# Row kurtosis of a 1024 x 8192 matrix: unequal folded groups replaced by 32 equal groups in a hand-set order

## The chip, the cores and the metric

The kernel runs on one core of one Trainium2 chip. The time is device time in microseconds (us) of one execution; three executions of the kernel before were timed, and one more was profiled.

## The reference

For each of the 1024 rows of x (8192 numbers, float32) the kernel returns the excess kurtosis.

```python
mean = np.mean(x, axis=-1, keepdims=True)
std = np.std(x, axis=-1, keepdims=True)
z = (x - mean) / (std + 1e-8)
return (np.mean(z ** 4, axis=-1) - 3).astype(np.float32)
```

Both kernels compute, per row, the mean, then S2, the sum of (x - mean)^2, then S4, the sum of (x - mean)^4, and return n * S4 / S2^2 - 3. The addition of 1e-8 is left out in both.

## The kernel before, in words

A group is a set of rows that fills the 128 partitions. With a fold of k, each row is cut in k pieces that lie on k neighbouring partitions, so that a group has 128/k rows and its tile is 128 x (8192/k). PLAN (line 15) lists the 24 groups in order: folds 8, 8, 4, then thirteen groups of fold 2 (64 rows, tile 128 x 4096, 2 MB), then 4, 4, 8, 8, 16, 16, 16, 16. Each group passes through these steps:

- one load of the whole tile from SP's queue (line 188), into one of a few slots for its width (10 for fold 2);
- the mean. For folds 4 and more, VectorE adds up each partition (line 96) and TensorE adds the pieces of a row with a block matrix (line 103). For fold 2, TensorE transposes the tile in 128 x 128 pieces, all accumulated into one PSUM tile `tps` (line 123: 32 matmuls for a tile of 4096 columns), VectorE adds the k neighbours and spreads the sum over them in one reduction to `red` (line 129, which reads each value k times), and TensorE adds over the partitions with a column of -1/n (line 134);
- ScalarE copies the negative mean `nmu` from PSUM (lines 105, 137);
- ScalarE squares (x + nmu) in place and sums into a column of `sa` (line 192), followed by its own read of the accumulator. This is called the square below;
- the fourth power: a square of the square with a sum, on VectorE (line 175), or on ScalarE (line 171) for every fifth group (groups 2, 7, 12, 17, 22); half each for the last group.

Groups of one fold that stand next to each other form a batch (six of them). At the end of a batch two sums over the pieces go through TensorE (`p2`, `p4`, lines 151 to 153), four small VectorE instructions form the result (lines 155 to 160), and it is stored, from ScalarE's queue but for the last batch.

The order of the instructions on each engine is set by the framework's scheduler and not by the code: it places the next group's transposes, for instance, partly ahead of line 134 of the group before. `psum` has two buffers of `tps` and of `mps`, `psfin` one of `p2` and of `p4`.

Of the kernel before, what the change touches and what calls it, by code (L numbers as in the profile page):

```python
# [7 lines left out]
f32 = mybir.dt.float32  # L8
bf16 = mybir.dt.bfloat16
AO = mybir.AluOpType  # L10
AF = mybir.ActivationFunctionType
P = 128


PLAN = [8, 8, 4, 2, 2, 2, 2, 2, 2, 2, 2, 2, 2, 2, 2, 2, 4, 4, 8, 8, 16, 16, 16, 16]
SLOTS = {2: 10, 4: 2, 8: 2, 16: 4}


@with_exitstack
def kernel(  # L20
    ctx: ExitStack,
    tc: tile.TileContext,
    x: bass.AP,
    out: bass.AP,
):
    nc = tc.nc
    n_rows, n_cols = x.shape
    neg_inv_n = -1.0 / float(n_cols)
    assert sum(P // k for k in PLAN) == n_rows

    xpool = ctx.enter_context(tc.tile_pool(name="xpool", bufs=1))
    const = ctx.enter_context(tc.tile_pool(name="const", bufs=1))
    junkp = ctx.enter_context(tc.tile_pool(name="junkp", bufs=1))
    small = ctx.enter_context(tc.tile_pool(name="small", bufs=6))
    fin = ctx.enter_context(tc.tile_pool(name="fin", bufs=2))
    psum = ctx.enter_context(tc.tile_pool(name="psum", bufs=2, space=bass.MemoryType.PSUM))
    psfin = ctx.enter_context(tc.tile_pool(name="psfin", bufs=1, space=bass.MemoryType.PSUM))


    warm = const.tile([P, 1], f32, name="warm")  # L40
    nc.vector.memset(warm, 0.0)
    nc.scalar.activation(out=warm, in_=warm, func=AF.Square)


    blk = {}

    def block_matrix(k):
        if k not in blk:
            r = P // k
            b = const.tile([P, P], f32, name=f"blk{k}")  # L50
            v = b.rearrange("p (r k) -> p r k", k=k)
            nc.gpsimd.memset(b, neg_inv_n)
            nc.gpsimd.affine_select(  # L53
                out=v, in_=v, pattern=[[-k, r], [0, k]], base=0,
                channel_multiplier=1, compare_op=AO.is_ge, fill=0.0,
            )
            nc.gpsimd.affine_select(  # L57
                out=v, in_=v, pattern=[[k, r], [0, k]], base=k - 1,
                channel_multiplier=-1, compare_op=AO.is_ge, fill=0.0,
            )  # L60
            blk[k] = b
        return blk[k]

    for k in PLAN:
        block_matrix(k)

    groups = []
    row = 0
    for k in PLAN:
        groups.append((row, k, P // k, n_cols // k))  # L70
        row += P // k


    batches = []
    for i, g in enumerate(groups):
        if batches and groups[batches[-1][0]][1] == g[1] and len(batches[-1]) < 64:
            batches[-1].append(i)
        else:
            batches.append([i])
    where = {}  # L80
    for b in batches:
        n = len(b)
        sa = const.tile([P, 2 * n], f32, name=f"sa{b[0]}")
        sd = const.tile([P, n], f32, name=f"sd{b[0]}")
        nc.gpsimd.memset(sa, 0.0)
        nc.gpsimd.memset(sd, 0.0)
        for j, i in enumerate(b):
            where[i] = (b, j, n, sa, sd)

    junk = junkp.tile([P, 1024], bf16, name="junk")  # L90

    def mean_dve(i, xt):
        row, k, r, w = groups[i]
        h = w // 2
        part = small.tile([P, 1], f32, name="part")
        nc.vector.tensor_tensor_reduce(  # L96
            out=junk[:, :h], in0=xt[:, :h], in1=xt[:, h:],
            scale=neg_inv_n if k == 1 else 1.0, scalar=0.0,
            op0=AO.add, op1=AO.add, accum_out=part)
        if k == 1:  # L100
            return part
        mps = psum.tile([P, 1], f32, name="mps")
        nc.tensor.matmul(mps, lhsT=blk[k], rhs=part, start=True, stop=True)  # L103
        nmu = small.tile([P, 1], f32, name="nmu")
        nc.scalar.copy(nmu, mps)  # L105
        return nmu

    ident = const.tile([P, P], f32, name="ident")
    nc.gpsimd.memset(ident, 1.0)
    nc.gpsimd.affine_select(  # L110
        out=ident, in_=ident, pattern=[[-1, P]], base=0,
        channel_multiplier=1, compare_op=AO.is_equal, fill=0.0)
    negcol = const.tile([P, 1], f32, name="negcol")
    nc.gpsimd.memset(negcol, neg_inv_n)

    def mean(i, xt):
        row, k, r, w = groups[i]
        if k > 2:
            return mean_dve(i, xt)
        ch = w // P  # L120
        tps = psum.tile([P, P], f32, name="tps")
        for c in range(ch):
            nc.tensor.matmul(tps, lhsT=xt[:, c * P:(c + 1) * P], rhs=ident,  # L123
                             start=c == 0, stop=c == ch - 1, is_transpose=True)
        red = small.tile([P, P], f32, name="red")
        if k == 1:
            nc.vector.tensor_copy(red, tps)
        else:
            nc.vector.tensor_reduce(  # L129
                out=red.rearrange("p (r k) -> p r k", k=k),  # L130
                in_=tps.rearrange("p (r k) -> p r k", k=k).unsqueeze(2).to_broadcast([P, r, k, k]),
                op=AO.add, axis=mybir.AxisListType.X)
        mps = psum.tile([P, 1], f32, name="mps")
        nc.tensor.matmul(mps, lhsT=red, rhs=negcol,  # L134
                         start=True, stop=True)
        nmu = small.tile([P, 1], f32, name="nmu")
        nc.scalar.copy(nmu, mps)  # L137
        return nmu

    def split(i, w):  # L140
        if i == len(groups) - 1:
            return w // 2
        return w if i % 5 == 2 else 0

    def finish_batch(b):
        _, _, n, sa, sd = where[b[0]]
        row, k, r, w = groups[b[0]]
        sel = blk[k].rearrange("p (r k) -> p r k", k=k)[:, :, 0]
        p2 = psfin.tile([n, r], f32, name="p2")
        p4 = psfin.tile([n, r], f32, name="p4")  # L150
# [3 lines left out]
        rec = fin.tile([n, r], f32, name="rec")
        nc.vector.reciprocal(rec, p2)  # L155
        kr = fin.tile([n, r], f32, name="kr")
        nc.vector.scalar_tensor_tensor(  # L157
            out=kr, in0=p4, scalar=-1.0, in1=rec, op0=AO.mult, op1=AO.mult)
        nc.vector.tensor_mul(kr, kr, rec)  # L159
        nc.vector.tensor_scalar_add(kr, kr, -3.0)  # L160
        dst = out[row:row + n * r].rearrange("(g r) -> g r", r=r)
        eng = nc.sync if b is batches[-1] else nc.scalar
        eng.dma_start(out=dst, in_=kr)  # L163

    def fourth(i):
        row, k, r, w = groups[i]
        b, j, n, sa, sd = where[i]
        xt = tiles[i]
        cl = split(i, w)
        if cl > 0:  # L170
            nc.scalar.activation(  # L171
                out=xt[:, :cl], in_=xt[:, :cl], func=AF.Square,
                accum_out=sa[:, n + j:n + j + 1])
        if cl < w:
            nc.vector.tensor_tensor_reduce(  # L175
                out=xt[:, cl:], in0=xt[:, cl:], in1=xt[:, cl:], scale=1.0, scalar=0.0,
                op0=AO.mult, op1=AO.add, accum_out=sd[:, j:j + 1])
        if j == n - 1:
            finish_batch(b)

    tiles = {}
    used = {}
    for i, (row, k, r, w) in enumerate(groups):
        s = used.get(w, 0)
        used[w] = s + 1
        xt = xpool.tile([P, w], f32, name=f"x{k}", tag=f"x{k}_{s % SLOTS[k]}")
        tiles[i] = xt
        nc.sync.dma_start(
            out=xt, in_=x[row:row + r, :].rearrange("r (k w) -> (r k) w", k=k))
        nmu = mean(i, xt)  # L190
        b, j, n, sa, sd = where[i]
        nc.scalar.activation(  # L192
            out=xt, in_=xt, func=AF.Square, bias=nmu, accum_out=sa[:, j:j + 1])
        if i > 0:
            fourth(i - 1)
    fourth(len(groups) - 1)


# [28 lines left out]
```

## Time and profile before

| what | value |
|---|---|
| median of the three timed runs | 134.7 us (134.06 to 134.92) |
| the profiled execution: its own time | 134.22 us |
| span of that execution, first to last instruction | 132.5 us |
| busy: VectorE (DVE) | 73.6 us, 56% |
| busy: ScalarE (ACT) | 80.2 us, 61% |
| busy: TensorE (PE), matmuls | 74.8 us, 56% |
| loaded from HBM | 33.55 MB |

The span is part of the execution's own time; 1.72 us lie around it. Busy shares are means over stages that differ, so the rows below go by stages and by single steps. PEclk is the clock that TensorE was granted, 1.00 for 2.4 GHz and 0.50 for 1.2 GHz.

### The profile page before, as it was taken

The numbers are of one execution on the slowest core, as the hardware profiler recorded it, in microseconds if no ns is written. First come the engines' busy times: TensorE is split into PE (matmuls) and PEld (weight loads), VectorE is DVE, ScalarE is ACT, GpSimd is POOL, SyncE is SP. The second block draws the span as 40 slices with busy tenths as digits, with TensorE's granted clock in tenths as the row PEclk, the third lists the DMA queues.
The fourth block names the chain that finished last, engine by engine and source line by source line (L and its number), as shares of the span: only waits on it lengthen the run. The fifth ranks groups of instructions, "written<-read, shape, count | busy, mean of one in ns | idle before, by whom it ended". The sixth has DMA issues, their size and how long they took to land. (4 is left out here: it accounts for less than half of the span.)

```text
span 132.5 us, 1379 instructions
## 1 busy us (share of the span) xinstructions
PE 74.8 (56%) x500; PEld 69.0 (52%) x500; DVE 73.6 (56%) x98; ACT 80.2 (61%) x86; POOL 5.8 (4%) x31
## 2 busy tenths in 40 slices
PE   0223999419894298789403989168999202115430
PEld 0221989319794297779303979067989101014420
DVE  0458011580299709610996069931015999998881
ACT  4076608309292196999901948047899694449890
POOL 8900000000000000000000000000000000000000
PEclk9999999985699959999995599965589975555555
DMA  4999999999999999999999996000000000000000
GB/s 114 433 462 415 420 445 401 425 435 401 465 406 450 415 435 435 401 460 406 455 406 406 419 403 232 0 2 0 0 0 7 0 0 0 0 0 1 0 0 0
DMA packets 3511, 33.64 MB, mean 254 GB/s; under 512 B 433, under 2 KB 433, under 8 KB 1457
## 3 DMA queue, kind: packets, MB, share of 16 engines
q1 hardware_dynamic: 3464, 33.56, 60.5%
q8 instruction: 4, 0.07, 0.2%
q14 instruction: 3, 0.02, 0.0%
q10 hardware_dynamic: 40, 0.00, 0.0%
HBM read 33.55 MB, written 0.00 MB: 253 GB/s over the span
## 5 line engine op out<-in xcount | busy, mean ns | idle before, releaser
L175 DVE CUSTOM_DVE_ANT_0 x<-x 128x4096 f32<-128x4096 f32 (+4 forms) x19 | 57.4, 3027 | 10.1 <-ACT x L192 5.0
L192 ACT ACTIVATE x<-x,nmu 128x4096 f32<-128x4096 f32 (+3 forms) x24 | 61.7, 2573 | 1.3 <-DVE kr L160 0.6
L123 PE MATMUL tps<-ident,x 128*128 128x128 f32 x416 | 61.2, 318 | 0.3 <-DMA x<-in_x_dram 0.3
L123 PEld LDWEIGHTS tps<-ident,x 128*128 128x128 f32 x416 | 59.6, 172 | 0.4 <-issue 0.4
L129 DVE TENSOR_REDUCE red<-tps 128x128 f32<-128x256 f32 x13 | 5.5, 423 | 38.2 <-PE tps L123 38.2
L137 ACT COPY nmu<-mps 128x1 f32<-128x1 f32 x13 | 2.0, 155 | 36.0 <-PE mps L134 36.0
L134 PE MATMUL mps<-negcol,red 128*128 128x1 f32 x26 | 5.5, 282 | 27.4 <-DVE red L129 27.4
L134 PEld LDWEIGHTS mps<-negcol,red 128*128 128x128 f32 x26 | 4.7, 225 | 30.5 <-issue 19.1
L171 ACT ACTIVATE x<-x 128x2048 f32<-128x2048 f32 (+3 forms) x6 | 12.1, 2013 | 0.9 <-DVE rec L155 0.8
L103 PE MATMUL mps<-part,blk 128*128 128x1 f32 x22 | 6.1, 358 | 10.5 <-DVE part L96 10.5
L103 PEld LDWEIGHTS mps<-part,blk 128*128 128x128 f32 x22 | 5.4, 315 | 11.6 <-issue 7.7
L96 DVE CUSTOM_DVE_ANT_0 junk<-x 128x512 bf16<-128x512 f32 (+2 forms) x11 | 8.1, 737 | 5.7 <-DMA x<-in_x_dram 5.7
L105 ACT COPY nmu<-mps 128x1 f32<-128x1 f32 x11 | 1.4, 153 | 10.4 <-PE mps L103 10.4
L151 PE MATMUL p<-blk,sa 128*2 128x16 f32 (+4 forms) x12 | 1.6, 218 | 10.4 <-ACT x L192 8.7
L151 PEld LDWEIGHTS p<-blk,sa 128*2 128x2 f32 (+3 forms) x12 | 0.6, 85 | 11.0 <-ACT x L192 9.1
L153 PE MATMUL p<-blk,sd 128*2 128x16 f32 (+4 forms) x12 | 1.6, 222 | 5.4 <-DVE sd L175 5.3
L192 ACT ACTIVATION_READ_ACCUMULATOR x<-x,nmu 128x1 f32 x24 | 4.5, 187 | 0.0
L153 PEld LDWEIGHTS p<-blk,sd 128*2 128x2 f32 (+3 forms) x12 | 0.8, 92 | 5.7 <-DVE sd L175 4.0
L57 POOL TENSOR_SCALAR_AFFINE_SELECT blk<-blk 128x128 f32<-128x128 f32 x4 | 2.1, 545 | 0.0
L155 DVE RECIPROCAL rec<-p 2x16 f32<-2x16 f32 (+4 forms) x6 | 1.9, 317 | 0.3 <-PE p L151 0.2
L152 PE MATMUL p<-blk,sa 128*2 128x16 f32 (+4 forms) x12 | 1.5, 206 | 1.0 <-ACT x L171 0.8
L53 POOL TENSOR_SCALAR_AFFINE_SELECT blk<-blk 128x128 f32<-128x128 f32 x4 | 1.9, 501 | 0.0
(20 smaller groups left out, 11.5 us busy)
## 6 DMA issues: line engine op xcount, KB each, us to landing
x<-in_x_dram SPq DMA_DIRECT2D x13, 2048.0 KB, 27.9
x<-in_x_dram SPq DMA_DIRECT2D x3, 1024.0 KB
x<-in_x_dram SPq DMA_DIRECT2D x4, 512.0 KB, 3.9
x<-in_x_dram SPq DMA_DIRECT2D x4, 256.0 KB, 14.4
out_dram<-kr ACTq DMA_DIRECT2D x3, 0.1 KB
out_dram<-kr ACTq DMA_DIRECT2D x1, 3.2 KB
out_dram<-kr ACTq DMA_DIRECT2D x1, 0.2 KB
out_dram<-kr SPq DMA_DIRECT2D x1, 0.1 KB
```

The costliest lines, as they stand in the source:

```text
L57: nc.gpsimd.affine_select(out=v, in_=v, pattern=[[k, r], [0, k]], base=k - 1, channel_multiplier=-1, compare_op=AO.is_ge, fill=0.0,)
L96: nc.vector.tensor_tensor_reduce(out=junk[:, :h], in0=xt[:, :h], in1=xt[:, h:], scale=neg_inv_n if k == 1 else 1.0, scalar=0.0, op0=AO.add ...
L103: nc.tensor.matmul(mps, lhsT=blk[k], rhs=part, start=True, stop=True)
L123: nc.tensor.matmul(tps, lhsT=xt[:, c * P:(c + 1) * P], rhs=ident, start=c == 0, stop=c == ch - 1, is_transpose=True)
L129: nc.vector.tensor_reduce(out=red.rearrange("p (r k) -> p r k", k=k), in_=tps.rearrange("p (r k) -> p r k", k=k).unsqueeze(2).to_broadcast ...
L134: nc.tensor.matmul(mps, lhsT=red, rhs=negcol, start=True, stop=True)
L137: nc.scalar.copy(nmu, mps)
L151: nc.tensor.matmul(p2, lhsT=sa[:, 0:n], rhs=sel, start=True, stop=True)
L153: nc.tensor.matmul(p4, lhsT=sd, rhs=sel, start=False, stop=True)
L171: nc.scalar.activation(out=xt[:, :cl], in_=xt[:, :cl], func=AF.Square, accum_out=sa[:, n + j:n + j + 1])
L175: nc.vector.tensor_tensor_reduce(out=xt[:, cl:], in0=xt[:, cl:], in1=xt[:, cl:], scale=1.0, scalar=0.0, op0=AO.mult, op1=AO.add, accum_out ...
L192: nc.scalar.activation(out=xt, in_=xt, func=AF.Square, bias=nmu, accum_out=sa[:, j:j + 1])
```

## The change

All rows are now in 32 equal groups of 32 rows, folded over K = 4 partitions: a tile is 128 x 2048 (1 MB), loaded in two pieces of 1024 columns (512 KB each), and there are 24 slots. All loads are issued first in SP's queue; the three stores follow on the same queue.

Every group takes the way by transposes: 16 matmuls into `tps`; VectorE adds the 4 neighbours to `part` (128 x 32) in one instruction and spreads `part` to `red` (128 x 128) in a second one; TensorE forms the mean, ScalarE copies it and squares. The fourth powers of groups 3, 9, 15, 21 and 27 are on ScalarE, the others on VectorE; the last group's 2048 columns are cut at 1152 (ScalarE the first part). `manual_schedule()` keeps the instructions of each engine in the order in which the code emits them: for group i the transposes, the reduction and the spreading, the mean, the square, VectorE's fourth power of group i - 1, and then ScalarE's of group i if it is one of the five. The batches are groups 0 to 25, 26 to 30, and 31. The first is finished within group 28. For the other two, 1/S2^2 is formed ahead of the last fourth power.

```diff
-PLAN = [8, 8, 4, 2, 2, 2, 2, 2, 2, 2, 2, 2, 2, 2, 2, 2, 4, 4, 8, 8, 16, 16, 16, 16]
-SLOTS = {2: 10, 4: 2, 8: 2, 16: 4}
+K = 4
+GROUPS = 32
+CHUNK = 1024
+SLOTS = 24
+ACT_EVERY = 6
+LAST_ACT_S4 = 1152
+LAG_BATCH = 26
...
+    ctx.enter_context(tc.manual_schedule())
...
+    batches = [list(range(LAG_BATCH)), list(range(LAG_BATCH, GROUPS - 1)), [GROUPS - 1]]
...
+    def load(i):
+        xt = xpool.tile([P, W], f32, name="xt")
+        xts[i] = xt
+        src = x[i * R:(i + 1) * R, :].rearrange("r (k w) -> (r k) w", k=K)
+        for c in range(0, W, CHUNK):
+            nc.sync.dma_start(out=xt[:, c:c + CHUNK], in_=src[:, c:c + CHUNK])
+
+    def turn(i):
+        tps = psum.tile([P, P], f32, name="tps")
+        tpss[i] = tps
+        for c in range(0, W, P):
+            nc.tensor.matmul(tps, lhsT=xts[i][:, c:c + P], rhs=ident,
+                             start=c == 0, stop=c == W - P, is_transpose=True)
+
+    def reduce(i):
+        red = small.tile([P, P], f32, name="red")
+        reds[i] = red
+        part = small.tile([P, R], f32, name="part")
+        nc.vector.tensor_reduce(
+            out=part, in_=tpss[i].rearrange("p (r k) -> p r k", k=K), op=AO.add, axis=AX)
+        nc.vector.tensor_copy(
+            red.rearrange("p (r k) -> p r k", k=K), part.unsqueeze(2).to_broadcast([P, R, K]))
+
+    def mean(i):
         mps = psum.tile([P, 1], f32, name="mps")
+        nc.tensor.matmul(mps, lhsT=reds[i], rhs=negcol, start=True, stop=True)
         nmu = small.tile([P, 1], f32, name="nmu")
         nc.scalar.copy(nmu, mps)
...
+    def second_moment(b):
+        j, n, sa, sd = where[b[0]]
+        p2 = psfin.tile([n, R], f32, name="p2")
         nc.tensor.matmul(p2, lhsT=sa[:, 0:n], rhs=sel, start=True, stop=True)
+        rec = fin.tile([n, R], f32, name="rec")
+        nc.vector.reciprocal(rec, p2)
+        rec2 = fin.tile([n, R], f32, name="rec2")
+        nc.vector.scalar_tensor_tensor(
+            out=rec2, in0=rec, scalar=-1.0, in1=rec, op0=AO.mult, op1=AO.mult)
+        return rec2
+
+    def finish(b, rec2):
+        j, n, sa, sd = where[b[0]]
+        p4 = psfin.tile([n, R], f32, name="p4")
         nc.tensor.matmul(p4, lhsT=sa[:, n:2 * n], rhs=sel, start=True, stop=False)
         nc.tensor.matmul(p4, lhsT=sd, rhs=sel, start=False, stop=True)
+        kr = fin.tile([n, R], f32, name="kr")
+        nc.vector.tensor_mul(kr, p4, rec2)
         nc.vector.tensor_scalar_add(kr, kr, -3.0)
+        dst = out[b[0] * R:(b[0] + n) * R].rearrange("(g r) -> g r", r=R)
+        nc.sync.dma_start(out=dst, in_=kr)
+
+    L = GROUPS - 1
+    for i in range(GROUPS):
+        load(i)
+    for i in range(GROUPS):
+        turn(i)
+        reduce(i)
+        mean(i)
+        square(i)
+        if i >= 1 and (i - 1) % ACT_EVERY != 3:
+            fourth_dve(i - 1, 0)
+        if i < L and i % ACT_EVERY == 3:
+            fourth_act(i, W)
+        if i == LAG_BATCH + 2:
+            finish(batches[0], second_moment(batches[0]))
+    rec2 = second_moment(batches[1])
+    rec2l = second_moment(batches[2])
+    fourth_act(L, LAST_ACT_S4)
+    fourth_dve(L, LAST_ACT_S4)
+    finish(batches[1], rec2)
+    finish(batches[2], rec2l)
```

`square`, `fourth_act` and `fourth_dve` hold the same instructions as lines 192, 171 and 175 of the kernel before.

## Rows read from the trace of the kernel before

**Rows 1.** The page, busy tenths in 40 slices of 3.3 us: VectorE, ScalarE.

```profile
DVE  0458011580299709610996069931015999998881
ACT  4076608309292196999901948047899694449890
```

**Rows 2.** Windows by stage: stretch, us, each engine's busy us (instructions), PEclk, DMA share, GB/s.

```profile
13.00:81.40 68.40, 48.44 (x340) 46.25 (x341) 33.98 (x26) 40.25 (x30) 0.00 (x0) 0.88 1.00 423
81.40:130.40 49.00, 23.87 (x149) 20.85 (x146) 33.61 (x58) 33.50 (x46) 0.00 (x0) 0.66 0.01 2
```

**Rows 3.** Timeline, fold-2 groups at PEclk 1.00: start us, us, engine, line, tiles, count, [idle before].

```profile
49.99 0.42 DVE L129 TENSOR_REDUCE red<-tps 128x128 f32<-128x256 f32 x1 [4.55 <-PE tps L123]
50.33 4.42 DVE L175 CUSTOM_DVE_ANT_0 x<-x 128x4096 f32<-128x4096 f32 x1
...
51.14 3.72 ACT L192 ACTIVATE x<-x,nmu 128x4096 f32<-128x4096 f32 x1
...
54.67 0.42 DVE L129 TENSOR_REDUCE red<-tps 128x128 f32<-128x256 f32 x1
...
54.98 3.63 ACT L171 ACTIVATE x<-x 128x4096 f32<-128x4096 f32 x1
...
55.45 3.69 PE L123 MATMUL tps<-ident,x 128*128 128x128 f32 x32
58.51 0.19 ACT L171 ACTIVATION_READ_ACCUMULATOR x<-x 128x1 f32 x1
...
58.77 3.72 ACT L192 ACTIVATE x<-x,nmu 128x4096 f32<-128x4096 f32 x1
59.18 0.42 DVE L129 TENSOR_REDUCE red<-tps 128x128 f32<-128x256 f32 x1 [4.09 <-PE tps L123]
...
59.97 4.45 PE L123 MATMUL tps<-ident,x 128*128 128x128 f32 x39
```

**Rows 4.** Timeline, the same steps at PEclk 0.50.

```profile
29.83 5.79 PE L123 MATMUL tps<-ident,x 128*128 128x128 f32 x26
...
86.72 0.42 DVE L129 TENSOR_REDUCE red<-tps 128x128 f32<-128x256 f32 x1
...
87.70 4.51 PE L123 MATMUL tps<-ident,x 128*128 128x128 f32 x20
```

**Rows 5.** Groups by line and shape: instructions, then busy us, mean ns, idle before them.

```profile
L192 ACT ACTIVATE x<-x,nmu 128x2048 f32<-128x2048 f32 x3 | 6.0, 2002 | 0.2
...
L171 ACT ACTIVATE x<-x 128x2048 f32<-128x2048 f32 x2 | 3.8, 1910 | 0.8 <-DVE rec L155 0.8
...
L175 DVE CUSTOM_DVE_ANT_0 x<-x 128x2048 f32<-128x2048 f32 x1 | 2.3, 2270 | 0.0
...
L155 DVE RECIPROCAL rec<-p 1x32 f32<-1x32 f32 x1 | 0.3, 345 | 0.2 <-PE p L151 0.2
...
L159 DVE TENSOR_TENSOR kr<-kr,rec 2x16 f32<-2x16 f32 x2 | 0.3, 160 | 0.0
...
L159 DVE TENSOR_TENSOR kr<-kr,rec 13x64 f32<-13x64 f32 x1 | 0.2, 208 | 0.0
```

**Rows 6.** Windows around stretches in which TensorE ran or stood: columns as in Rows 2.

```profile
24.60:29.30 4.70, 0.00 (x0) 0.00 (x0) 4.70 (x3) 0.00 (x0) 0.00 (x0) 0.95 1.05 443
...
36.40:41.30 4.90, 4.90 (x45) 4.69 (x44) 4.66 (x3) 3.98 (x3) 0.00 (x0) 1.00 1.01 431
87.70:92.20 4.50, 4.50 (x21) 4.11 (x21) 0.00 (x0) 3.96 (x3) 0.00 (x0) 0.50 0.01 2
93.20:98.80 5.60, 5.60 (x34) 5.43 (x35) 0.00 (x0) 5.39 (x4) 0.00 (x0) 0.65 0.00 0
```

**Rows 7.** Timeline at the start: the steps that waited for the first two loads, 512 KB each.

```profile
4.29 0.83 DVE L96 CUSTOM_DVE_ANT_0 junk<-x 128x512 bf16<-128x512 f32 x1 [3.36 <-DMA x<-in_x_dram]
...
5.64 0.69 DVE L96 CUSTOM_DVE_ANT_0 junk<-x 128x512 bf16<-128x512 f32 x1 [0.51 <-DMA x<-in_x_dram]
```

**Rows 8.** Timeline at the end: the issue of the last store.

```profile
130.41 0.35 SPq L163 DMA_DIRECT2D out_dram<-kr  x1
```

More of the change, by code (lines that the diff above doesn't have):

```diff
@@ L42 @@
     nc.scalar.activation(out=warm, in_=warm, func=AF.Square)
[L45 to L79, printed above, removed]
+    ident = const.tile([P, P], f32, name="ident")
+    nc.gpsimd.memset(ident, 1.0)
+    nc.gpsimd.affine_select(
+        out=ident, in_=ident, pattern=[[-1, P]], base=0,
+        channel_multiplier=1, compare_op=AO.is_equal, fill=0.0)
+    negcol = const.tile([P, 1], f32, name="negcol")
+    nc.gpsimd.memset(negcol, neg_inv_n)
+    sel = const.tile([P, R], f32, name="sel")
+    nc.gpsimd.memset(sel, neg_inv_n)
+    nc.gpsimd.affine_select(
+        out=sel, in_=sel, pattern=[[-K, R]], base=0,
+        channel_multiplier=1, compare_op=AO.is_ge, fill=0.0)
+    nc.gpsimd.affine_select(
+        out=sel, in_=sel, pattern=[[K, R]], base=K - 1,
+        channel_multiplier=-1, compare_op=AO.is_ge, fill=0.0)
+    one = const.tile([1, 1], f32, name="one")
+    nc.gpsimd.memset(one, 1.0)
+    batches = [list(range(LAG_BATCH)), list(range(LAG_BATCH, GROUPS - 1)), [GROUPS - 1]]
     where = {}
@@ L87 @@
         for j, i in enumerate(b):
[L88 to L101, printed above, removed]
+            where[i] = (j, n, sa, sd)
@@ new lines @@
+    xts = {}
+    tpss = {}
+    reds = {}
+    mpss = {}
+    def load(i):
[10 more added lines that the diff above has]
+                             start=c == 0, stop=c == W - P, is_transpose=True)
@@ L102, in mean_dve @@
+    def reduce(i):
[7 more added lines that the diff above has]
+    def mean(i):
         mps = psum.tile([P, 1], f32, name="mps")
-        nc.tensor.matmul(mps, lhsT=blk[k], rhs=part, start=True, stop=True)
+        nc.tensor.matmul(mps, lhsT=reds[i], rhs=negcol, start=True, stop=True)
@@ L104, in mean_dve @@
         nmu = small.tile([P, 1], f32, name="nmu")
         nc.scalar.copy(nmu, mps)
[L106 to L150, printed above, removed]
-        nc.tensor.matmul(p2, lhsT=sa[:, 0:n], rhs=sel, start=True, stop=True)
+        mpss[i] = nmu
+    def square(i):
+        j, n, sa, sd = where[i]
+        nc.scalar.activation(out=xts[i], in_=xts[i], func=AF.Square, bias=mpss[i],
+                             accum_out=sa[:, j:j + 1])
@@ new lines, in fourth_act, with fourth_dve @@
+    def fourth_act(i, c):
+        j, n, sa, sd = where[i]
+        nc.scalar.activation(out=xts[i][:, :c], in_=xts[i][:, :c], func=AF.Square,
+                             accum_out=sa[:, n + j:n + j + 1])
+    def fourth_dve(i, c):
+        j, n, sa, sd = where[i]
+        nc.vector.tensor_tensor_reduce(
+            out=xts[i][:, c:], in0=xts[i][:, c:], in1=xts[i][:, c:], scale=1.0, scalar=0.0,
+            op0=AO.mult, op1=AO.add, accum_out=sd[:, j:j + 1])
+    def second_moment(b):
+        j, n, sa, sd = where[b[0]]
+        p2 = psfin.tile([n, R], f32, name="p2")
+        nc.tensor.matmul(p2, lhsT=sa[:, 0:n], rhs=sel, start=True, stop=True)
+        rec = fin.tile([n, R], f32, name="rec")
[4 more added lines that the diff above has]
+        return rec2
@@ L152, in finish_batch @@
+    def finish(b, rec2):
+        j, n, sa, sd = where[b[0]]
+        p4 = psfin.tile([n, R], f32, name="p4")
         nc.tensor.matmul(p4, lhsT=sa[:, n:2 * n], rhs=sel, start=True, stop=False)
         nc.tensor.matmul(p4, lhsT=sd, rhs=sel, start=False, stop=True)
[L154 to L158, printed above, removed]
@@ L159, in finish_batch @@
-        nc.vector.tensor_mul(kr, kr, rec)
-        nc.vector.tensor_scalar_add(kr, kr, -3.0)
[L161 to L195, printed above, removed]
@@ L196 @@
-    fourth(len(groups) - 1)
+        kr = fin.tile([n, R], f32, name="kr")
+        nc.vector.tensor_mul(kr, p4, rec2)
+        nc.vector.tensor_scalar_add(kr, kr, -3.0)
+        dst = out[b[0] * R:(b[0] + n) * R].rearrange("(g r) -> g r", r=R)
[14 more added lines that the diff above has]
+            finish(batches[0], second_moment(batches[0]))
```

12 lines of the change are left out of this document (7 added, 5 removed).

## The prediction, as put on record before the result

> **What bounds the kernel now.** First the page's slices: both arithmetic engines have gaps through the first 25 slices and are dense only at the end [rows 1]. Then the same by stage: from 13.0 to 81.4 us the loads run at full share, 423 GB/s, while VectorE works 34.0 of 68.4 us and ScalarE 40.3; after the loads there are 49 us more, in which each works 33.6 of 49.0 [rows 2]. So no engine and no transfer is full all the way. Third, the timeline shows why: it is a round trip. VectorE reduces `tps`, TensorE forms the mean and begins the next group's transposes, and VectorE's next reduction waits 4.09 us for their end [rows 3]; at the lower clock the same 32 transposes take nearly twice as long [rows 4]. What was not done under the loads is done after them. The chain of waits covers only the last 5 us and adds nothing.
>
> **The change part by part.** The arithmetic stays: 8192 x 1024 numbers are squared on ScalarE, and fourth powers split much as before. What changes is the size of a round (16 transposes in place of 32), and that each engine's order is fixed. So I sum one round, and then what comes before, between and after 31 of them.
>
> *One round, from one reduction's start to the next.* At PEclk 1.00, 39 transposes take 4.45 us and 32 take 3.69, so 0.109 each, and 16 take 3.69 - 16 x 0.109 = 1.95. From the reduction's end (54.67 + 0.42 = 55.09) to the first transpose at 55.45 is 0.36, the mean's matmul included; from the last transpose's end (59.14) to the next reduction is 0.04 [rows 3]. That is 2.35 us.
> VectorE's two instructions are not in the trace. The reduction reads 128 values where the old one reads 256 in 0.42; small operations give about 1.0 ns per value over some 0.145 (0.160 for 16 values, 0.208 for 64) [rows 3, 5]. I take 0.29 (bounds 0.21 and 0.42) for reading 128, and 0.28 for writing 128 in the spreading copy (bounds 0.16, the 16-value row, and 0.42), with 0.04 between them, as from TensorE to VectorE. The pair is 0.61 (0.41 to 0.88), and one round 0.61 + 2.35 = 2.96 us.
> The Trainium skill, "VectorE: DVE Perf Modes", section "Mode 2×_2P", says that a float32 copy from SBUF to SBUF handles two elements a cycle, because no second tensor takes the other read port. By that the copy would be an estimated 0.07 us shorter, and the whole sum 2.1 us less, 116.6 us; no row here has such a copy.
>
> *What lies under a round.* VectorE must fit the fourth power of the group before: 2.27 us, of which the last 0.08 overlaps the next instruction (50.33 + 4.42 against 54.67), so 2.19, and with the pair, whose end overlaps by as much, 2.72 [rows 3, 5]. ScalarE's round is 2.16: the square takes 2.00, its accumulator read starts 0.10 before its end, and the next square follows 0.26 after that start (58.51 to 58.77) [rows 3, 5]. A load of 1 MB takes 2.5 us at 423 GB/s [rows 2]. All three fit in 2.96, barely. The square starts 0.73 after the pair (50.41 to 51.14), so 1.34 after the reduction's start, and is read out at 3.43; VectorE asks for it at 2.96 + 0.53 = 3.49. Cover: 0.06 us; where it is gone, each us costs a us.
>
> *The five fourth powers on ScalarE.* They take 1.9 us each off VectorE's list, but VectorE isn't the bound, so they gain nothing, and they sit ahead of the next square. Counted from group 3's reduction: its square is read out at 3.43, the fourth power starts at 3.46, its read at 5.27, the square of group 4 at 5.53 in place of 4.30, read out at 7.65. VectorE is in order: it waits at group 4's fourth power from 6.45 to 7.65, and behind that stands the reduction of group 6, which starts at 7.65 + 2.19 = 9.84 and not 8.88. Each costs 0.96 us, five 4.8. ScalarE has caught up two rounds later. The finish of batch 0 (two sums on TensorE, four small VectorE instructions, about 0.9 us) stands in group 28, where VectorE has no fourth power: the wait of 1.2 us after group 27 hides it; uncovered it costs 0.9.
>
> *The start.* The first 512 KB is there at 4.29, the second at 5.64 [rows 7], before the eighth transpose needs it. I cost the first transposes at the lower clock, since TensorE has stood until then, as it had before the run at 29.83 [rows 4, 6]. At PEclk 0.50, 26 transposes take 5.79 and 20 take 4.51, so 0.213 each, and 16 take 4.51 - 4 x 0.213 = 3.66 [rows 4]. The first reduction is at 4.29 + 0.10 + 3.66 + 0.04 = 8.1 us. A round at this clock is 0.61 + (87.70 - 87.14 = 0.56) + 3.66 + 0.04 = 4.87, so 1.91 longer.
> How many rounds stay cold? After a run of 5.8 us from 29.83 the next stretch is at 1.00, and a run begun at 93.2 reached the higher clock on its way (mean 0.65); one of 4.5 us from 87.70 did not [rows 4, 6]. Here runs of 3.66 us alternate with 1.2 us. I take two cold rounds after the first transposes, 3.8 us (bounds none and five, 0 and 9.6).
>
> *The end.* From the last reduction: 0.61, less the overlap, and the fourth power of group 30 to 2.72; a reciprocal (0.35) and a product (0.17) for batch 1 to 3.28; the last square is read out at 3.43, its sum on TensorE some 0.4; reciprocal and product again, to 4.4; only then the last fourth power on VectorE, 896 of 2048 columns, about 1.1, to 5.5 (ScalarE's 1152 columns end by 4.8); four small products and sums and TensorE's last sum, 0.9, to 6.4 [rows 3, 5]. The last store's issue to the end of the span is 132.5 - 130.41 = 2.1 [rows 8]: 8.5 us.
>
> *Costed at nothing.* The loads: 64 issues on SP, each about 0.35 like the store's [rows 8], are 22 us beside 81; the slot of group i + 24 is free long before. The stores leave ScalarE's queue for SP's, where they stand behind the loads; only the last is waited for. The trace speaks on the smaller transfers: the second 512 KB landed 1.35 us after the first, 388 GB/s, near the 423 of 2 MB ones [rows 2, 7]. The Trainium skill, "DMA: Bandwidth & Descriptors", section "Measured (HBM→SBUF, 128 partitions, SWDGE, issued from GpSimd)", speaks against this: transfers should be 1 MiB or more to reach three quarters of the peak. The row, at 92% of the larger transfers' rate, disagrees with it for transfers that follow each other in the queue.
>
> **The sum.** 8.1 + 31 x 2.96 (91.8) + 4.8 + 3.8 + 8.5 = 117.0 us of span, and with the 1.7 us that lie around it (134.2 less 132.5) 118.7. The profiled execution's 134.2 stands 0.5 us under the median of 134.7, which is nothing here.
>
> **Rivals.**
> (a) The clock stays low. Mechanism: the 1.2 us in each cold round in which TensorE waits for VectorE and the mean are enough to keep it at 0.50. Then rounds are 4.87, ScalarE's 2.16 + 1.9 fits within, and the time is 8.1 + 31 x 4.87 + 8.5 + 1.7 = 169 us, slower. It decides from ten cold rounds on: 114.9 + 10 x 1.91 = 134. For it: the 4.5 us run that did not raise the clock. Against: that run was followed by one that did, after a gap of only 1.0 us [rows 6].
> (b) The clock rises but falls again in the waits behind ScalarE's fourth powers, where TensorE stands for about 1.7 us. Five falls with two cold rounds each are 5 x 3.8 = 19: 138 us. Against: the fall of [rows 6] came only late in 4.7 us of standing (mean 0.95).
> (c) The round trip is hidden, if transposes run ahead of the mean as the scheduler's order let them. Then the last load lands at 5.6 + 31 x 2.45 = 81.6, its transposes end 2 us later, and the end adds 8.5 + 1.7: 94 us. Against: the code emits a group's mean ahead of the next transposes.
> (d) The smaller transfers don't overlap: at most 4.3 us each, as the first one's landing counted from the span's start, up to 64 x 4.3 + 10 = 285 us. Against: the second one's 1.35 us [rows 7].
>
> **How the numbers follow.** Forecast 0.81, (a) 0.07, (b) 0.06, (c) 0.05, (d) 0.01. The forecast's bounds: the pair at 0.41 gives 31 x 0.20 = 6 less, at 0.88 8 more; cold rounds 4 less or 6 more. Not all fall on one side: 110 to 129 is the range, and leaves out the rivals, which together hold 0.19. A measurement of this kernel can tell about 1% from no change. Faster by over 1% (under 133.4): the forecast but for its far end, and (c), 0.85; within 1%: 0.04; slower: (a), (b) mostly, (d), 0.11.
>
> **What would show it.** Right: reductions some 2.96 us apart, VectorE waiting for TensorE before each and TensorE for VectorE's copy before each mean; one wait of about 1.2 us for ScalarE two groups after each of groups 3, 9, 15, 21, 27; PEclk 0.50 for two or three groups and 1.00 from then on; loads done by about 82 us and waited for nowhere after the first group. Wrong: PEclk 0.50 in the middle slices; a pair far from 0.61; VectorE's waits at fourth powers in every round, which would make ScalarE's lag and not TensorE the bound; or loads that land later than their group's turn.

## The result, and the profile after

The changed kernel takes 119.29 us (median of four timed executions, 119.15 to 123.12) against 134.41 us before (four, 134.06 to 134.92), a ratio of 0.8869 with a 95% interval of 0.8825 to 0.8913. The profiled execution took 119.15 us, its span is 117.4 us. The ratios, here and below, leave out executions more than 1.5% above the fastest of their kernel, here the one of 123.12 us, which ran at a mean granted clock of 0.90 against 0.93 to 0.94 of the others.

From the page after: busy tenths in 40 slices of 2.9 us, then the chain that ended last, shares of the span by engine.

```profile
PE   0387777776797777376777477777767777777110
...
DVE  0011999159548924989961899991593998479971
ACT  5007777995374799577799877789953779995760
...
PEclk9999999998559999999999999999976999999995
DMA  3999999999999999999999999999910000000000
...
DMA 32%; DVE 20%; PE 18%; ACT 18%; issue 8%; SPq 1%; ACTq 0%; DVEq 0%
```

Against [rows 1] the work is spread evenly, with no dense block left at the end. The chain goes through VectorE, TensorE and ScalarE in nearly equal parts, which is what a ring (a closed round of handovers, in which each engine waits for the one before it) looks like from outside: none of them is the bound alone. The third that it gives to loads is its first 40 us, and is not to be taken at its word: TensorE waited for a load once, 4.9 us before the first transposes.

One round and one wait behind a fourth power on ScalarE, from the timeline after: start, us, engine, line, what, [idle before, released by].

```profile
11.28 0.29 DVE L103 TENSOR_REDUCE part<-tps 128x32 f32<-128x128 f32 x1 [2.34 <-PE tps L96]
11.60 0.23 DVE L105 COPY red<-part 128x128 f32<-128x128 f32 x1
...
11.88 0.38 PE L110 MATMUL mps<-negcol,red 128*128 128x1 f32 x2 [0.64 <-DVE red L105]
11.94 2.29 DVE L127 CUSTOM_DVE_ANT_0 xt<-xt 128x2048 f32<-128x2048 f32 x1
...
12.13 1.94 PE L96 MATMUL tps<-ident,xt 128*128 128x128 f32 x16
...
14.16 0.28 DVE L103 TENSOR_REDUCE part<-tps 128x32 f32<-128x128 f32 x1
...
20.45 1.91 ACT L122 ACTIVATE xt<-xt 128x2048 f32<-128x2048 f32 x1
...
22.54 2.01 ACT L117 ACTIVATE xt<-xt,nmu 128x2048 f32<-128x2048 f32 x1
...
24.66 2.29 DVE L127 CUSTOM_DVE_ANT_0 xt<-xt 128x2048 f32<-128x2048 f32 x1 [1.27 <-ACT nmu L112]
...
26.88 0.29 DVE L103 TENSOR_REDUCE part<-tps 128x32 f32<-128x128 f32 x1
...
27.57 0.35 PE L110 MATMUL mps<-negcol,red 128*128 128x1 f32 x2 [1.88 <-DVE red L105]
```

The transposes of group 2 start at 12.13 and end at 14.07; VectorE reduces at 14.16. Most reductions are 2.89 or 2.90 us apart. Group 3's fourth power at 20.45 makes group 4's square late (22.54), VectorE waits 1.27 us for it, and the reduction of group 6 starts at 26.88, 4.04 after the one before (22.84). The steps are those of [rows 3]. TensorE meanwhile stands, that is, runs no matmul, for 1.88 us.

The two new VectorE instructions, by line and shape: instructions, then busy us, mean ns, idle before.

```profile
L127 DVE CUSTOM_DVE_ANT_0 xt<-xt 128x2048 f32<-128x2048 f32 x26 | 59.6, 2293 | 6.6 <-ACT nmu L112 6.0 <-issue 0.3
...
L103 DVE TENSOR_REDUCE part<-tps 128x32 f32<-128x128 f32 x32 | 9.3, 291 | 26.4 <-PE tps L96 25.0
...
L105 DVE COPY red<-part 128x128 f32<-128x128 f32 x32 | 7.2, 227 | 1.1
```

The granted clock, from windows of the trace after: stretch, us, busy us of TensorE's matmuls, of its weight loads, of VectorE, ScalarE and GpSimd, PEclk, DMA share, GB/s.

```profile
10.00:25.70 15.70, 12.06 (x102) 10.76 (x100) 10.32 (x17) 13.75 (x18) 0.00 (x0) 1.00 1.03 413
25.80:27.50 1.70, 0.00 (x0) 0.00 (x0) 1.67 (x5) 1.00 (x2) 0.00 (x0) 1.00 1.02 410
28.50:35.30 6.80, 6.06 (x30) 5.57 (x28) 3.89 (x6) 4.01 (x5) 0.00 (x0) 0.50 1.03 411
...
35.35:86.55 51.20, 35.04 (x293) 31.58 (x292) 38.34 (x61) 41.41 (x54) 0.00 (x0) 1.00 1.00 399
...
84.50:86.20 1.70, 0.00 (x0) 0.00 (x0) 1.67 (x5) 0.97 (x2) 0.00 (x0) 1.00 0.49 198
86.50:89.90 3.40, 3.40 (x17) 3.14 (x17) 1.82 (x2) 2.26 (x3) 0.00 (x0) 0.51 0.03 10
```

The clock is at 1.00 from the second group on, falls twice, each time after TensorE stood behind one of ScalarE's fourth powers, and comes back. It does not fall after the stands of the same 1.88 us that end at 48.99 and 67.72, which lie in the stretch 35.35 to 86.55, nor after the fifth, of 1.50, that ends at 106.4.

The sum of the prediction beside what the trace after shows, in us of span:

| term | forecast | measured |
|---|---|---|
| first reduction starts | 8.1 | 8.38 |
| 31 rounds | 31 x 2.96 = 91.8 | 31 x 2.895 = 89.7 |
| waits behind five fourth powers of ScalarE | 5 x 0.96 = 4.8 | 5 x 1.15 = 5.8 |
| rounds at PEclk 0.50 at the start | 3.8 | 0 |
| rounds at 0.50 later | 0 | 4.5 |
| from the last reduction to the end | 8.5 | 8.8 |
| sum | 117.0 | 117.2 (span 117.4) |

The 4.5 are what the rounds that end at 30.81, 35.57 and 90.08 are longer than 2.895 (1.03, 1.87, 1.64). The fifth wait is spread over two rounds, 3.27 and 3.67, since the first batch's finish lies in the first of them. One round of 3.12 us at 54.30 makes up the missing 0.2.

Where the 15 us come from: not from a shorter round for the same rows. The shortest rounds before take 4.5 us for 64 rows at PEclk 1.00 [rows 3], and two of the changed kernel's take 5.8. But from the first to the last of the thirteen reductions before, twelve rounds average 7.15 us (4.5 to 12.1), 85.8 for 768 rows; 24 rounds of the changed kernel at their mean of 3.23, waits and low clock included, are 77.6, so 8.2 less. The other 256 rows and both ends take 46.7 us before and 39.8 now, 6.9 less. The first and the last of these reductions before, then after:

```profile
19.47 0.42 DVE L129 TENSOR_REDUCE red<-tps 128x128 f32<-128x256 f32 x1 [6.33 <-PE tps L123]
...
105.25 0.42 DVE L129 TENSOR_REDUCE red<-tps 128x128 f32<-128x256 f32 x1
```

```profile
8.38 0.29 DVE L103 TENSOR_REDUCE part<-tps 128x32 f32<-128x128 f32 x1 [7.45 <-PE tps L96]
...
108.59 0.29 DVE L103 TENSOR_REDUCE part<-tps 128x32 f32<-128x128 f32 x1
```

### The profile page after: what moved, and what is told of

Read it like the earlier page. It is cut to its first block, busy times and chain, and to the rows that moved or that the text cites. A ratio compares the mean times of both kernels' runs of the same rounds, so it can differ in the third digit from the quotient of the medians.

```text
span 117.4 us, 1705 instructions
## 1 busy us (share of the span) xinstructions
PE 76.6 (65%) x594; PEld 69.0 (59%) x594; DVE 78.2 (67%) x131; ACT 83.8 (71%) x110; POOL 1.6 (1%) x17
## 4 chain that ended last, share of the span: by engine, by line
DMA 32%; DVE 20%; PE 18%; ACT 18%; issue 8%; SPq 1%; ACTq 0%; DVEq 0%
DMA xt<-in_x_dram 32%; ACT xt L117 15%; PE tps L96 14%; DVE xt L127 13%; PE mps L110 4%; DVE part L103 3%; DVE red L105 3%; ACT xt L122 2%; SPq L90 1%; ACT nmu L112 1%; DVE rec L137 1%; DVE kr L149 0%; PE p L135 0%; DVE kr L150 0%; PE p L146 0%
## 5 line engine op out<-in xcount | busy, mean ns | idle before, releaser
L96 PE MATMUL tps<-ident,xt 128*128 128x128 f32 x512 | 68.1, 291 | 4.9 <-DMA xt<-in_x_dram 4.9
L96 PEld LDWEIGHTS tps<-ident,xt 128*128 128x128 f32 x512 | 63.5, 156 | 4.9 <-issue 4.8
L117 ACT ACTIVATE xt<-xt,nmu 128x2048 f32<-128x2048 f32 x32 | 64.2, 2005 | 1.4 <-ACT nmu L112 0.2
L127 DVE CUSTOM_DVE_ANT_0 xt<-xt 128x2048 f32<-128x2048 f32 (+1 forms) x27 | 60.7, 2248 | 6.6 <-ACT nmu L112 6.0
L110 PEld LDWEIGHTS mps<-negcol,red 128*128 128x128 f32 x64 | 9.7, 191 | 36.2 <-ACT xt L117 26.3
L110 PE MATMUL mps<-negcol,red 128*128 128x1 f32 x64 | 11.5, 250 | 29.1 <-DVE red L105 29.1
L103 DVE TENSOR_REDUCE part<-tps 128x32 f32<-128x128 f32 x32 | 9.3, 291 | 26.4 <-PE tps L96 25.0
L122 ACT ACTIVATE xt<-xt 128x2048 f32<-128x2048 f32 (+1 forms) x6 | 10.7, 1787 | 0.2
L105 DVE COPY red<-part 128x128 f32<-128x128 f32 x32 | 7.2, 227 | 1.1
L117 ACT ACTIVATION_READ_ACCUMULATOR xt<-xt,nmu 128x1 f32 x32 | 5.9, 186 | 0.0
## 6 DMA issues: line engine op xcount, KB each, us to landing
xt<-in_x_dram SPq DMA_DIRECT2D x64, 512.0 KB, 10.2
```

The lines of the kernel that those rows point to most:

```text
L96: nc.tensor.matmul(tps, lhsT=xts[i][:, c:c + P], rhs=ident, start=c == 0, stop=c == W - P, is_transpose=True)
L103: nc.vector.tensor_reduce(out=part, in_=tpss[i].rearrange("p (r k) -> p r k", k=K), op=AO.add, axis=AX)
L105: nc.vector.tensor_copy(red.rearrange("p (r k) -> p r k", k=K), part.unsqueeze(2).to_broadcast([P, R, K]))
L110: nc.tensor.matmul(mps, lhsT=reds[i], rhs=negcol, start=True, stop=True)
L117: nc.scalar.activation(out=xts[i], in_=xts[i], func=AF.Square, bias=mpss[i], accum_out=sa[:, j:j + 1])
L122: nc.scalar.activation(out=xts[i][:, :c], in_=xts[i][:, :c], func=AF.Square, accum_out=sa[:, n + j:n + j + 1])
```

## The experiments

Each changes the kernel after the change unless it says otherwise. Median and range are of all its executions; ratios are to the kernel before, on the same chip.

| label | edit | median us (range) | ratio (95% interval) |
|---|---|---|---|
| e1_no_act | no fourth power on ScalarE but the last group's share | 111.93 (109.72 to 113.55) | 0.8177 (0.8105 to 0.8249) |
| e2_warm | idle TensorE filled behind ScalarE's fourth powers | 116.93 (116.27 to 118.44) | 0.8689 (0.8625 to 0.8753) |
| e4_one_red | one reduction in place of reduction and copy | 124.06 (123.0 to 124.99) | 0.9209 (0.9121 to 0.9298) |
| e8_lag2 | VectorE's fourth power two groups behind | 112.49 (111.58 to 113.35) | 0.8309 (0.8237 to 0.8382) |
| e3_ahead | transposes ahead of the mean | 116.08 (115.5 to 117.12) | 0.8689 (0.8633 to 0.8745) |
| e7_both | e3 and e8 together | 102.2 (102.06 to 102.33) | 0.7642 (0.7622 to 0.7663) |
| e5_no_order | no hand-set order | 124.15 (123.96 to 125.95) | 0.9279 (0.925 to 0.9308) |
| e6_chunk | loads of 1 MB | 122.01 (119.62 to 125.34) | none given |
| e9_no_act_warm | e1, TensorE busy before the first load lands | 108.97 (108.84 to 109.36) | 0.8112 (0.806 to 0.8164) |
| e10_warm_all | e2, TensorE busy before the first load lands | 114.13 (114.03 to 128.94) | 0.8483 (0.8431 to 0.8535) |
| e11_both_1mb | e7 with loads of 1 MB but for the first group | 101.33 (101.07 to 102.13) | 0.758 (0.7527 to 0.7632) |

**What VectorE does between transposes and mean is on every round (e4).**

```diff
-        part = small.tile([P, R], f32, name="part")
-        nc.vector.tensor_reduce(
-            out=part, in_=tpss[i].rearrange("p (r k) -> p r k", k=K), op=AO.add, axis=AX)
-        nc.vector.tensor_copy(
-            red.rearrange("p (r k) -> p r k", k=K), part.unsqueeze(2).to_broadcast([P, R, K]))
+        nc.vector.tensor_reduce(
+            out=red.rearrange("p (r k) -> p r k", k=K),
+            in_=tpss[i].rearrange("p (r k) -> p r k", k=K).unsqueeze(2).to_broadcast([P, R, K, K]),
+            op=AO.add, axis=AX)
```

> One reduction that reads each value four times (512 values) in place of the reduction and the copy, as the kernel before did with 256. Theory (what VectorE does between transposes and mean is on every round): by 1.04 ns a value the pair of 0.56 becomes about 0.69, 31 x 0.13 = 4.0 us more, 123 us. Rival (VectorE has time to spare and the round is set elsewhere): 119 us.

From its groups by line and shape:

```profile
L102 DVE TENSOR_REDUCE red<-tps 128x128 f32<-128x512 f32 x32 | 22.1, 691 | 30.4 <-PE tps L96 28.3
```

0.69 us as worked out, and the undisturbed rounds are 3.03 to 3.04 long, 0.14 more. 31 x 0.14 is 4.3, and the time is 4 to 6 us above the changed kernel's 119.2. The length of the undisturbed rounds is the measure here, since other terms move too: in the profiled execution rounds at 0.50 cost 7.4 us and not 4.5, and the waits behind ScalarE's fourth powers 0.87 each and not 1.15. VectorE waits for TensorE 28.3 us in all, and still each tenth of a microsecond of VectorE's work is paid for 31 times: an engine with idle time can be the bound if it stands inside the ring.

**ScalarE's five fourth powers hold the kernel up (e1).**

```diff
-        if i >= 1 and (i - 1) % ACT_EVERY != 3:
+        if i >= 1:
             fourth_dve(i - 1, 0)
-        if i < L and i % ACT_EVERY == 3:
-            fourth_act(i, W)
```

> All fourth powers but the last group's share go to VectorE. Theory (a round is set by TensorE's round trip, 2.89 us, and ScalarE's five fourth powers only hold up VectorE): VectorE's 0.56 + 2.22 fits in the round, so the five waits of 1.15 us go (5.8 us) and with them the long stands of TensorE and the clock falls behind them (4.5 us); the first batch's finish is uncovered (0.5 to 0.9 more): about 110 us. Rival (VectorE is the bound and ScalarE relieves it): five more fourth powers of 2.2 us, about 130 us.

VectorE now does 11 us more and the kernel takes 109.7 to 113.6 us and not 119.2. Rounds are 2.90 from the third on, no wait of 1.15 is left, and the round with the batch's finish is 3.69 (0.79 uncovered, where 0.9 was costed). The expected 110 is met by two of the five executions (109.72, 109.96); the profiled one, 113.55, has two rounds of 4.81 and 4.55 at the start, 3.6 too many. Its timeline for TensorE and its windows:

```profile
9.68 3.65 PE L96 MATMUL tps<-ident,xt 128*128 128x128 f32 x16
```

```profile
8.50:17.50 9.00, 7.62 (x36) 7.22 (x36) 3.34 (x6) 4.51 (x6) 0.00 (x0) 1.00 1.02 400
17.60:106.00 88.40, 63.80 (x535) 57.39 (x533) 84.29 (x126) 67.49 (x90) 0.00 (x0) 1.00 0.79 314
```

Read with care: the windows say PEclk 1.00 for 8.5 to 17.5 us, while 16 transposes take 3.65 us, the low level's price in [rows 4]. The trace's first record of the clock is at 17.56, and what lies ahead of it is shown as 1.00.

**The waits come from the order, not from ScalarE's load (e8).**

```diff
-        if i >= 1 and (i - 1) % ACT_EVERY != 3:
-            fourth_dve(i - 1, 0)
+        if i >= 2 and (i - 2) % ACT_EVERY != 3:
+            fourth_dve(i - 2, 0)
...
+    fourth_dve(L - 1, 0)
     rec2 = second_moment(batches[1])
```

> VectorE's fourth power follows two groups behind the square in place of one. Theory (the wait of 1.2 us behind each of ScalarE's fourth powers comes from the fixed order, with the late square asked for too early): the waits go (5.8 us) and the clock falls behind them (4.5 us), rounds stay 2.89, and one more fourth power stands at the end (1.5 to 2.2): about 111 us. Rival (ScalarE has too much work with five fourth powers, whatever the order): 118 us or more.

VectorE's waits, all of them over 0.5 us: waited for, us in total, times, longest.

```profile
DVE part L103 <- PE tps L96: 25.8, 8, 7.7
DVE warm L47 <- PEq L189: 0.9, 1, 0.9
```

The waits for ScalarE (6.0 us, five times, in the changed kernel) are gone with ScalarE's work untouched, the rounds are 2.90, and PEclk stays 1.00 from 13.0 us to behind the last round. The expected 111 is nearly met by two executions (111.58, 111.64); the other two take 113.34 and 113.35, and the latter, which was profiled, has one round of 4.69 at the start, 1.8 too long.

**What the clock's falls cost (e2, e10, e9).**

```diff
+    dum = psfin.tile([P, P], f32, name="dum")
...
         turn(i)
+        if i % ACT_EVERY == 0 and i > 0:
+            for _ in range(14):
+                nc.tensor.matmul(dum, lhsT=ident, rhs=ident, start=True, stop=True,
+                                 is_transpose=True)
         reduce(i)
```

> 14 further transposes of the identity, which nothing reads, fill most of TensorE's stand of 1.88 us in groups 6, 12, 18, 24 and 30. Theory (the two falls of the clock after such stands cost 4.5 us): no stretch at 0.50 between the first transposes and the last group, about 114.7 us, rounds and the five waits as they were. Rival (the falls come from elsewhere, or cost nothing since other waits lie over them): 119 us and the same low stretches.

A window of its trace:

```profile
17.90:113.40 95.50, 71.65 (x610) 65.17 (x608) 74.44 (x121) 77.81 (x102) 0.00 (x0) 1.00 0.73 289
```

No fall any more, and the waits of 1.15 are as they were. But 116.3 to 118.4 us is only about 1 to 3 less, not 4.5, and misses the 114.7: in the profiled execution two rounds at the start, 4.81 and 4.67, give back 3.7. So e10 and e9 add 14 transposes that nothing reads ahead of group 0's, to e2 and to e1:

```diff
+    for _ in range(14):
+        nc.tensor.matmul(dum, lhsT=ident, rhs=ident, start=True, stop=True, is_transpose=True)
     for i in range(GROUPS):
         turn(i)
```

> The changed kernel with the filling transposes in groups 6, 12, 18, 24, 30 and the 14 ahead of the first group. Theory (rounds at 0.50 cost 4.5 us in the changed kernel's profiled execution, and what the filling alone left of that is the start): no round at 0.50, 114.7 us in every execution. Rival (the filling alone was short of 114.7 since the filling itself costs): 116 to 117 us.

> The kernel with all fourth powers on VectorE, and 14 transposes of the identity, which nothing reads, ahead of the first group's while TensorE waits for the first load. Theory (the spread of that kernel, 109.7 to 113.6 us, is the number of rounds at 0.50 at the start, up to two of 4.7 us): every execution at 109 to 110 us, the second reduction 2.9 us after the first. Rival (the spread comes from elsewhere): the same spread around 112 us.

e9 takes 108.84 to 109.36 us, as expected; e10 takes 114.03, 114.10 and 114.16, and a fourth time 128.94. But for that one, the changed kernel with the start and the stands filled is 5 us faster, and the spread of e1 is gone. (The three executions of e10 were not profiled, so that they hold no round at 0.50 is read from their time alone.) Not all of it is rounds at 0.50: in e9 the first group's transposes run faster too, and the first reduction is at 7.30 and not 8.56 as in e1. The second comes 3.25 after it and not 2.9, as TensorE's weight loads wait 0.37 us within group 1 for its second load. That leaves 0.9, by which e9 is under the best of e1. Every later round but the finish's is within 0.1 of 2.9.

The execution of 128.94 us is the one that was profiled, and it measures the ring once more. Window and timeline of TensorE:

```profile
6.90:122.00 115.10, 93.03 (x649) 82.86 (x649) 76.26 (x122) 81.69 (x107) 0.00 (x0) 0.75 0.70 278
```

```profile
40.20 0.35 PE L110 MATMUL mps<-negcol,red 128*128 128x1 f32 x2 [0.73 <-DVE red L105]
40.41 2.44 PE L96 MATMUL tps<-ident,xt 128*128 128x128 f32 x16
43.59 0.35 PE L110 MATMUL mps<-negcol,red 128*128 128x1 f32 x2 [0.74 <-DVE red L105]
```

The granted clock is 0.75 throughout, between the two levels. Sixteen transposes take 2.43 or 2.44 every time, in place of 1.94, and the rounds 3.39 in place of 2.90: the half microsecond goes into the round undiminished.

**A second ring lies just beneath the first (e3, e7).** e3 moves the transposes:

```diff
-        turn(i)
+        if i == 0:
+            turn(0)
         reduce(i)
+        if i < L:
+            turn(i + 1)
         mean(i)
```

> Only the transposes are moved ahead of the mean. Theory (a second ring lies just beneath: pair, mean, square, then the fourth power one group later, then the next pair, (3.41 + 2.22) / 2 = 2.82 us a round, and the waits behind ScalarE's fourth powers stay, about 1.3 each): 31 x 0.07 less and five times 0.2 more, 118 us, give or take 4 us of clock. Rival (the TensorE trip is the only ring): as with both changes, near 100 us.

> The transposes of group i + 1 are emitted ahead of the mean of group i, and VectorE's fourth power follows two groups behind. Theory (the round trip over TensorE sets the round, and once it and the chain square to fourth power are both loosened the work of the engines and the loads does): a round of about 2.5 us (ScalarE 2.16 + 1.9/6, VectorE 0.56 + 2.22 x 5/6, a load 2.45), 8.5 + 31 x 2.5 + 10.5 + 1.8 = 98 us, some 2 more where the start is at the low clock. Rival (something else of the same length holds the round at 2.9): 110 us or more.

VectorE's largest waits in e3, and three of its reductions:

```profile
DVE xt L127 <- ACT nmu L112: 14.7, 6, 3.9
DVE part L103 <- PE tps L96: 8.8, 2, 7.5
```

```profile
52.46 0.29 DVE L103 TENSOR_REDUCE part<-tps 128x32 f32<-128x128 f32 x1
...
55.18 0.28 DVE L103 TENSOR_REDUCE part<-tps 128x32 f32<-128x128 f32 x1
...
58.08 0.29 DVE L103 TENSOR_REDUCE part<-tps 128x32 f32<-128x128 f32 x1
```

Alone, the move takes away the waits for TensorE (25.0 us after, 8.8 here, of which 7.5 are the start) and puts waits for ScalarE in their place (6.0 after, 14.7 here): 116.1 us. The rounds are the second ring's: undisturbed they are mostly 2.68 to 2.72 and 2.90 to 2.94 by turns, so 2.81 on average where 2.82 was expected. With the fourth power two groups behind as well, e7 takes 102.2 us. Its VectorE timeline and TensorE's waits:

```profile
61.78 0.29 DVE L103 TENSOR_REDUCE part<-tps 128x32 f32<-128x128 f32 x1
...
64.47 0.28 DVE L103 TENSOR_REDUCE part<-tps 128x32 f32<-128x128 f32 x1
...
67.15 0.28 DVE L103 TENSOR_REDUCE part<-tps 128x32 f32<-128x128 f32 x1
```

```profile
PE tps L96 <- DMA xt<-in_x_dram: 9.3, 18, 5.0
...
PE mps L110 <- DVE red L105: 2.2, 2, 1.3
```

Rounds of 2.69 are VectorE's own work, back to back: the reduction 0.29, 0.03 to the copy, 0.15 from its start to the fourth power's, and 2.22 to the next reduction. Where VectorE has no fourth power, since ScalarE takes it, a round is as short as 0.8, and in the next, of 3.75, VectorE waits 1.0 us for ScalarE. So six rounds take 15.3 us, and from 54.60 to 69.84 ScalarE is busy for 14.89 of 15.24 us: with both rings open, ScalarE's own work is nearly the bound. The expected 98 us is missed by 4: the mean round is 2.63 and not 2.5, which is 31 x 0.13. From 119.3, e3 alone takes off 3 us, e8 alone 7, both together 17.

**The loads (e6, e11).**

```diff
-CHUNK = 1024
+CHUNK = 2048
```

> One load of 1 MB for each group in place of two of 512 KB. Theory (halving the transfers costs nothing, and only the first group gains from it): the first reduction 1.2 to 1.5 us later, loads done at the same time, all else the same, about 1.3 us more than the changed kernel. Rival (the smaller transfers lose rate): the loads end earlier than 85 us and the time is no longer than 119 us.

Windows of the changed kernel and then of e6, the stretch in which both load all the time:

```profile
6.00:81.00 75.00, 54.47 (x424) 49.40 (x423) 52.14 (x82) 56.82 (x74) 0.00 (x0) 0.95 1.03 407
```

```profile
6.00:81.00 75.00, 54.66 (x420) 49.62 (x421) 52.13 (x82) 56.02 (x73) 0.00 (x0) 0.95 1.01 422
```

The rival was half right: pieces of 512 KB load at 407 GB/s and not 422, and the last lands at 87.4 us where e6's lands at 84.1. Nothing waits for it. The first reduction is 0.98 later in e6 (9.36), and its profiled execution takes 119.62, 0.5 more than the changed kernel's where 1.3 was expected, since its rounds at 0.50 cost 0.2 less and one odd round of 3.12 is missing. Its four executions range from 119.62 to 125.34, so the time alone settles nothing.

In e7 TensorE waits for loads, so there the rate should matter:

```diff
-        for c in range(0, W, CHUNK):
-            nc.sync.dma_start(out=xt[:, c:c + CHUNK], in_=src[:, c:c + CHUNK])
+        chunk = CHUNK if i == 0 else W
+        for c in range(0, W, chunk):
+            nc.sync.dma_start(out=xt[:, c:c + chunk], in_=src[:, c:c + chunk])
```

> Transposes ahead of the mean and fourth powers two groups behind, with one load of 1 MB for each group but the first. Theory (in that kernel the loads set the pace, and whole groups load at 422 GB/s against 407): the loads end near 84 us and not 87, and the time falls from 102.2 to 99 to 100.5 us. Rival (the engines set the pace, and the few waits for loads are covered): 102 us, the same.

Windows of e11:

```profile
6.00:81.00 75.00, 63.02 (x517) 59.00 (x516) 59.76 (x99) 66.52 (x88) 0.00 (x0) 0.98 1.01 421
81.00:90.00 9.00, 6.72 (x61) 6.16 (x61) 8.42 (x17) 8.84 (x15) 0.00 (x0) 1.00 0.21 87
```

The loads end at 84.9 us, 2.4 earlier, but the time is 101.3 and the interval of the ratio overlaps e7's: a miss. After 81 us ScalarE works 8.84 of 9 us and VectorE 8.42. What is left to compute then, and not the loads, ends the kernel. (The profiled execution, at 102.13 the slowest of the four, also has a stretch at 0.50 from 26.3 to 29.7 us that e7's has not, with a round of 5.15.) e7 and e11 are the fastest versions found.

**The hand-set order (e5).**

```diff
-    ctx.enter_context(tc.manual_schedule())
```

> The equal groups without the hand-set order: the framework's scheduler places the instructions. Theory (the smaller equal groups bring most of the gain, the order only its regular rounds): uneven rounds, about 115 to 124 us. Rival 1 (the order brings the gain): back towards 134 us. Rival 2 (the order costs, since the scheduler puts transposes ahead of means): under 112 us.

VectorE's and TensorE's waits:

```profile
DVE part L102 <- PE tps L95: 30.6, 15, 7.6
...
PE mps L109 <- DVE red L104: 14.2, 17, 1.8
```

124.15 us, at the far end of the range given. In the profiled execution, of 125.95, the reductions are 1.5 to 6.8 us apart, and PEclk changes eleven times. So of the 15 us between before and after, about 10 come with the equal groups and what goes with them (transposes for all, the two VectorE instructions, the loads, the batches) even in the scheduler's order, and 5 with the order; these 10 were not taken apart further. The order chosen still leaves the 17 us that e7 finds.

## Why the prediction was right, step by step

- **What bounds it, the ring.** Right. e4 and the rounds at 0.75 lengthen a round by just what they add inside the ring; e7 opens both rings, the undisturbed rounds become VectorE's own, and over six of them ScalarE is nearly full.
- **One round, 2.96.** Measured 2.895. The reduction is 0.291 against 0.29, the path over TensorE as summed; the copy is 0.227 against 0.28, which over 31 rounds is 1.6 us of the 2.1 by which the rounds were too long. The rule cited for the copy, from the Trainium skill, "VectorE: DVE Perf Modes", section "Mode 2×_2P", gave an estimated 0.07 less, so 0.21: the trace is nearer to it than to my value. The reductions fit it: 0.291 for 128 values, 0.423 for 256 before and 0.691 for 512 in e4 make 1.04 ns a value over 0.158, and with the same 0.158 the copy has 0.54 ns a value.
- **Five fourth powers on ScalarE gain nothing and cost 0.96 each.** Right in mechanism: the wait is 1.27 against 1.20, its price 1.15. Group 6's reduction comes 9.84 us after group 3's, as forecast (by the forecast's own terms the read-out at 7.65 is 7.62, a slip that changes little); the difference is the shorter round, since three undisturbed rounds are 8.69 and not 8.88. e1 shows that they gain nothing, e8 that the fixed order is what makes them costly. The batch's finish was hidden as said; uncovered, in e1, it costs 0.79.
- **The start and the clock: the step that was wrong.** "I take two cold rounds after the first transposes": the profiled execution had none, others (e1, e2) had two, e4 and e8 one. It differs from execution to execution and lies inside the bounds given, but the rows that the forecast names do not fix the number. The first reduction, 8.38 against 8.1, is a small miss: the first transposes start at 4.86 and not 4.39, and take 3.48 and not 3.66.
- **"The fall came only late in 4.7 us of standing", put against rival (b): the other miss.** Of four stands of 1.88 us two were followed by a fall. Rival (b) was true in part, at 4.5 us and not the 19 it was priced at. The trace before had a sign of it that the forecast passes over, in windows of TensorE alone (stretch, us, busy us, PEclk, DMA share, GB/s): in a stand of 4.1 us the clock stays at 1.00, and it is at 0.50 in most of the run right behind it, as in the changed kernel.

```profile
41.40:45.50 4.10, 0.00 (x0) 1.00 1.03 440
45.80:49.90 4.10, 4.10 (x23) 0.58 1.04 444
```

- **The two errors on the clock, 3.8 too much at the start and 4.5 too little later,** nearly cancel, and so do the other terms (rounds 2.1 too much; waits, start and end 1.0, 0.3 and 0.3 too little). That the forecast of 118.7 lies so near is in part luck.
- **Rival (a), the clock low all along,** did not happen: the lowest mean granted clock of any execution is 0.757, in e10, and the low level lasted two rounds at most in the changed kernel's profile. **Rival (c),** transposes ahead and 94 us, did not happen since the code emits the mean first, as said; e3 shows that its price was wrong as well, because the second ring holds at 116.
- **Loads costed at nothing.** Right for the time, since nothing waits for them, but "loads done by about 82 us" was wrong: 87.4, at 407 GB/s. The rule of the Trainium skill, "DMA: Bandwidth & Descriptors", section "Measured (HBM→SBUF, 128 partitions, SWDGE, issued from GpSimd)", asks for 1 MiB or more to reach three quarters of the peak. It points the right way, smaller transfers lose rate; here, with several under way (a median of 10.2 us from issue to landing, one issued every 1.2 us), pieces of 512 KB lose only 3.6% against loads of 1 MB.
- **The end.** 8.8 against 8.5: the last result is formed 6.4 after the last reduction, as summed, and the store takes 2.4.

## What to carry to other kernels

Where several engines hand one group around, and none is full, sum the ring, not the engines: price one full round from handover to handover, and look for the next ring just beneath it, since loosening one alone gives only a part (3 and 7 us here, 17 for both). When the rings are open, look at the engines' own work again. In a fixed order, work given to an engine with spare time can still cost if it stands ahead of something that the ring waits for; ask the consumer to come a group later before moving work. A price that hangs on the granted clock is a range and not a number, unless TensorE is kept busy through its stands.

## What the runs showed of the hardware that was not expected

- A stand of TensorE of 1.9 us was enough for a fall to 0.50 in two of four cases in the changed kernel, where the falls of the kernel before came with stands of 4.1 us and more. What decides between them was not tried; filling 1.5 us of each stand removed every fall (e2's profiled execution).
- The number of low-clock rounds at the start varies by execution, two (e1, e2), one (e4, e8) or none (the changed kernel), and 14 transposes that nothing reads ahead of the first group removed them (e9: 108.84 to 109.36, against 109.72 to 113.55).
- In one execution of e10 the granted clock was 0.75 from its first record, at 6.8 us, to 122.9, neither of the two levels. What caused it is open.
